# The split weights of four MLPs start at shifting places of their tiles

## The chip, the cores and the metric

One core of one Trainium2 chip runs the whole program. The metric is the device time of that core in microseconds. An execution before the change took 3301.78 and 3303.79 us in the two runs shown; the median is 3302.78 us.

## What is computed

The reference is a float32 network in two blocks on 512 latent tokens (and 256 context tokens in the first block) of 1024 features. The first block has two layers of mixed attention (grouped heads, low-rank heads, a pooling branch), each followed by a squared-relu MLP. The second block has a dilated-attention layer and a gated recurrence, each followed by the same kind of MLP. So there are four MLPs of this form:

```python
def sq_relu_mlp(h, w1, w2):
    return jnp.square(jax.nn.relu(h @ w1)) @ w2      # w1: 1024 x 4096, w2: 4096 x 1024
```

The MLP of the first layer works on 768 tokens, the other three on 512.

## The kernel before

**Products in two parts.** Each float32 operand is split into a high part (type fp32r, a rounded copy) and a low part (the difference). A product is three matmuls, `mm3` (lines 159 to 163): high by high (line 161), high by low (162), low by high (163), all summed in one PSUM bank.

**Weights.** `wcols` and `wchunk` bring a chunk of 128x2048 numbers: one DMA into a raw tile `wr`, a ScalarE copy into `wh` (line 187), a VectorE subtraction into `wl` (line 188). Each of `wr`, `wh` and `wl` has two buffers, so chunk n waits for the matmuls of chunk n-2 to leave its buffers and then has the time of chunk n-1 to be ready. The first two chunks after `self.cut = 2` are cut into kt/2 pieces.

**The MLP** (`mlp`, line 469). In the up stage a chunk holds 256 hidden features (eight blocks of 128 rows, 256 columns each). The weights are the stationary operand, loaded 128 by 128, and the tokens `t` stream past them as the moving operand. The result goes through Relu and Square on ScalarE and is split into the tiles `t` of the hidden features. In the down stage a chunk holds 512 rows and 512 output columns, and the roles are exchanged: 128 tokens of hidden features are stationary, the weights stream by 512 columns. Eight rounds of `ups`, two down chunks, `ups` make one MLP: 16 up chunks and 16 down chunks. In the profile's names the moving operand stands first: `b<-t,wh` is the up stage, `b<-wh,t` the down stage; `b` and `s` are two kinds of PSUM tiles (the second block has only `b`).

**Counts from the loops.** First MLP, 768 tokens: down 6 x 2 x 4 x 3 x 8 = 1152 matmuls of 512 columns; up 14 chunks x 2 x 8 x 3 = 672 of 512 and as many of 256, and for the first two chunks, whose tokens come in three runs of 256, 288 more of 256: 960 of 256. Each of the other three MLPs: 768 down and 672 up of 512 columns, 192 up of 256.

**Where the tiles lie.** The pools are laid out one behind the other along each partition. In bytes of a partition: the two buffers of `wl` begin at 33952 and 43168, those of `wh` at 52384 and 61600, those of `wr` at 70816 and 79008. All of these are 32 bytes past a multiple of 128. The general tiles `t` begin at 134848 + 6144 n in the first block, 64 past a multiple of 128, and at 113056 + 4096 n in the second, 32 past one. Within the MLPs every block of an operand starts whole multiples of 512 bytes behind its tile's start. So in the first block the starts of weights and tokens differ by 32 bytes (modulo 64) and in the second block by none.

Of the kernel before, what the change touches and what calls it, by code (L numbers as in the profile page):

```python
# [8 lines left out]
F32 = mybir.dt.float32  # L9
# [19 lines left out]
# ---------------------------------------------------------------- constants of the shapes  # L29
# [81 lines left out]
class Net:  # L111
    def __init__(self, ctx, tc, t, out):
        self.ctx, self.tc, self.nc, self.t, self.out = ctx, tc, tc.nc, t, out
        pool = lambda name, bufs, **kw: ctx.enter_context(tc.tile_pool(name=name, bufs=bufs, **kw))
        self.cst = pool("cst", 1)
        self.wp = pool("wp", 2)
        self.wk = pool("wk", 2)
        self.pb = self.ps = None
        self.nbank = 0
        self.pend = []  # L120
        self.nev = 0
        self.fill = []
        self.cut, self.aid = 0, self.nc.vector
        self.cols = {}

    # ------------------------------------------------------------ small helpers
# [38 lines left out]
    def raw(self, tag="wr"):  # L165
        return self.wp.tile([128, 2048 if tag == "wr" else 2304], F32, tag=tag, name=tag)

    def wchunk(self, segs, kt, n):
        """Weights [kt*128, n] gathered from column segments (part slice, k slice, column, source)."""
        nc = self.nc  # L170
        f = lambda x: x.rearrange("p (k n) -> p k n", k=kt)
        hi = self.wp.tile([128, 2304], F32R, tag="wh", name="wh")[:, :kt * n]
        lo = self.wp.tile([128, 2304], F32R, tag="wl", name="wl")[:, :kt * n]
# [17 lines left out]
    def wcols(self, w, cols, kt=8):  # L191
        """Weights [kt*128, sum] from column ranges of w."""
        segs, at = [], 0
        for c0, c1 in cols:
            src = w[:, c0:c1].rearrange("(k p) n -> p k n", p=128)
            segs.append((slice(0, 128), slice(0, kt), at, src))
            at += c1 - c0
        return self.wchunk(segs, kt, at)

    # work put off by a number of ticks, so that no engine's queue holds it before its operands are there  # L200
# [13 lines left out]
    def need(self, *keys):  # L214
        """Emits all that was put off up to the last of keys (all of it without keys)."""
# [3 lines left out]
    def only(self, key):  # L219
        """Emits what was put off under one key, ahead of the rest."""  # L220
# [15 lines left out]
    def rsqrt_act(self, st, scale, eps):  # L236
        """The same where the tables of ScalarE are not in use for exponentials."""
# [3 lines left out]
    def split_to(self, hi, lo, src):  # L241
        """src (SBUF, full precision) into its two parts."""
# [7 lines left out]
    # ------------------------------------------------------------ setup  # L250
    def setup(self):
# [34 lines left out]
        # the parts of a modulation's row stand two partitions apart  # L286
# [17 lines left out]
    def load_cols(self, names, eng):  # L304
        """Vectors of features as columns, turned from rows."""
# [23 lines left out]
    # ------------------------------------------------------------ modulation  # L329
    def mod_load(self, i, u, tag="wr"):  # L330
        """Columns u*256.. of layer i's modulation weights, by 128 rows."""
# [13 lines left out]
    def mod_rows(self, ps, raw, more=False):  # L345
        """Four partial sums of the two rows of a modulation, 32 partitions apart."""
# [5 lines left out]
    def row_parts(self, out, ps):  # L352
        """Rows of a modulation, their high parts on partitions r of 32 and the low ones on r + 2."""
# [4 lines left out]
    def mod_unit(self, i, u):  # L358
        """Columns u*256.. of layer i's modulation: rows for a gate, else turned to per-feature columns."""
# [32 lines left out]
    def affine(self, i, which):  # L392
        """Per-feature factor and shift of the modulated norm, [128, 8, 2 (latent, context)]."""
# [21 lines left out]
    # ------------------------------------------------------------ norm and turn  # L415
    def turn(self, n, xh, xl, c0, a=None, b=None, every=2):
        """n (two halves of [128 tokens, 512]) to [feature, token] columns c0.. of the pair tiles, with factor and shift."""
# [26 lines left out]
    def kx(x, k, c0, n, step=1):  # L444
        """k-th 128 features of pair tiles x = (hi, lo), columns c0.."""
# [4 lines left out]
    def ssq(self, x, hf, ss):  # L450
        """Sum of squares of half hf of x into ss[:, hf]."""
# [16 lines left out]
    # ------------------------------------------------------------ squared-relu MLP  # L468
    def mlp(self, width, xT, w1, w2, ranges, tiles, sink, lag=3):
        nc = self.nc  # L470
        self.cut = 2
# [14 lines left out]
        def chunk():  # L486
            """The next 256 hidden features: weights, and tiles of their parts."""
            c0 = len(hs) * 256
            hs.append((self.slot([128, 2, width], F32R), self.slot([128, 2, width], F32R)))
            return hs[-1], self.wcols(w1, [(c0, c0 + 256)])  # L490
# [16 lines left out]
        for g in range(8):  # L507
# [3 lines left out]
            for c, (tt, c0) in self.skew(tiles, lag if g == 7 else len(tiles)):  # L511
                if w[c] is None:
                    w[c] = self.wcols(w2[g * 512:(g + 1) * 512], [(c * 512, c * 512 + 512)], kt=4)
                    self.pump()
# [9 lines left out]
    def skew(tiles, lag):  # L524
        """(0, tile) and (1, tile) over the tiles, the second following the first by lag tiles."""
# [6 lines left out]
    # ============================================================ first block  # L532
# [3 lines left out]
    def gains(self, i):  # L536
        """Head gains on every partition."""
# [3 lines left out]
        n = 0  # L541
# [8 lines left out]
    def tables(self, at, eng):  # L550
        """Rope tables with the head gains folded in."""
# [23 lines left out]
    def rope(self, dst, ps, nh, tab, tt, tmp):  # L575
        """dst = gains and (for latent tokens, over the last rw columns) rotation of nh heads."""
# [16 lines left out]
    def heads(self, ps, nh, w, tab, tt, out, sq, t1, t2):  # L593
        """Normed, gained, rotated heads of ps [128, nh*w] into out [128, nh, w]."""
# [9 lines left out]
    # ------------------------------------------------------------ attention over all tokens  # L604
    def attention(self, i, jobs):
        """jobs: dicts of prep (emits what the job needs, returns (kind, q, k, v)), mix tile, fill steps."""
# [4 lines left out]
        def ring(tag, n, width, size):  # L611
            """Space n of a ring of size in the tiles of weights, which are taken as they are needed."""
# [68 lines left out]
        def emit(v, u):  # L681
            """Scores of unit v between the turns and products of unit u."""
# [35 lines left out]
    def mix_parts(self, j, m):  # L718
        """Half m of a pair of mixed features that was kept whole, into its parts."""
# [7 lines left out]
    # ------------------------------------------------------------ one layer  # L727
    def enter(self, i):
        """Tiles of layer i's input, and the step that fills a token tile of them from the residual."""
# [11 lines left out]
    def first(self, cols):  # L741
        """First layer: its input and the first projection, a quarter of the features at a time as their modulation
        comes in. Returns the input tiles and the projection's sums."""
# [47 lines left out]
        def units(s):  # L791
            """Rows of the modulation of quarter s."""
# [8 lines left out]
        def columns(s):  # L801
            """The modulation's columns of quarter s."""
# [19 lines left out]
        def features(s, tp):  # L822
            """The parts of the features of quarter s of a pair of token tiles."""
# [59 lines left out]
    def layer(self, i, xT, tab, sums=None):  # L883
# [32 lines left out]
        # ckv | kr | cq (first half)  # L916
# [20 lines left out]
        # cq (second half) | q heads 0 3  # L937
# [21 lines left out]
        # k heads | v heads  # L959
# [6 lines left out]
        # q heads 1 4 2 5  # L966
# [5 lines left out]
        def stacked(src, toks, hi, lo=None):  # L972
            """Pairs of heads turned into parts over both halves of the rows: hi with lo, or (hi, lo) each twice."""
# [16 lines left out]
        # pool input; meanwhile the keys of the heads that share them  # L990
# [28 lines left out]
        # second projections of the latent-rank heads, a pair of heads at a time  # L1019
# [97 lines left out]
        # output projection, gated into the residual  # L1117
# [8 lines left out]
        def weights(c):  # L1126
            """A quarter of the output projection's columns, rows as the mixed features lie."""
# [111 lines left out]
    # ============================================================ second block  # L1239
# [5 lines left out]
    def ln_rows(self, name, i):  # L1245
        """Gain and shift of a layer norm on every partition."""
# [13 lines left out]
    def ln_turn(self, j, name, i, rows, xT, wait=2, table=True):  # L1260
        """Layer norm of token tile j: to feature-major parts, and in place as the next residual."""
# [19 lines left out]
        def finish():  # L1281
            """The last norm of token tile j, out to memory."""
# [40 lines left out]
    def project_out(self, w, mT, name, i):  # L1323
        """Output projection and the norm after it. Returns a function for the product of the first 768 mixed features and
        a quarter of the columns with a token tile, one that ends a token tile and norms it, and the tiles it fills."""
# [59 lines left out]
    # ------------------------------------------------------------ dilated attention  # L1385
    def dilated(self, xT):
# [10 lines left out]
        def project(r, order):  # L1397
            """Steps that project, rotate and turn the four heads of round r, two pairs; the tiles they fill."""
# [71 lines left out]
        def scores(T, hh, j):  # L1470
            """Masked scores of a head and block, exponentials and the sums' reciprocals; both heads of a pair at once."""
# [70 lines left out]
        held = (0, 1), (1, 0), (1, 1)  # places of the last steps of a round's projection in the units of the round  # L1542
# [38 lines left out]
        def unit(r, u, put, fill):  # L1581
            """Scores of unit u, the turns of the unit before it, the products of the one before that; steps between."""
# [51 lines left out]
    # ------------------------------------------------------------ gated recurrence  # L1634
    def hgrn(self, xT):
# [13 lines left out]
        def gates(h, pz, pq, key, f, q):  # L1649
# [7 lines left out]
            # log f over the whole range of f: one of the two factors is 1  # L1657
# [19 lines left out]
        def recur(h, qd, kd, kp, dec, box):  # L1677
            """The stages of one head's recurrence."""
# [67 lines left out]
        # weights in the order of their use: inputs of the first pair of heads, then gates, queries and inputs of each  # L1746
# [64 lines left out]
    def lower_bounds(self, rows):  # L1811
        nc = self.nc
        # lower bounds: the softmax over the two layers, second minus nothing of the first
# [74 lines left out]
```

## Time and profile before

| | us |
|---|---|
| median of the runs shown (2) | 3302.78 |
| lowest, highest | 3301.78, 3303.79 |
| span of the profiled execution | 3301.2 |
| TensorE busy in it | 3238.5 (98%) |
| VectorE busy | 1776.6 (54%) |
| ScalarE busy | 1265.7 (38%) |
| first MLP, from 406.8 | 576.4 |
| second MLP, from 1257 | 361.0 |
| third MLP, from 2319.7 | 360.3 |
| fourth MLP, from 2933.8 | 358.7 |

The profiled execution is told by its span, from its first to its last instruction; the page gives no other time of it. Matmuls overlap in the pipeline, so the duration of one is longer than the step from its start to the next start, and a busy TensorE says little. The rate is read in the timeline, as the time between two starts divided by the number of matmuls between them.

### The profile page before, as it was taken

The page shows a single profiled execution, that of the slowest core. Times are in us where ns is not written, and L with a number is a line of the kernel's source. Part 1 is how long each engine was busy: PE and PEld are TensorE (multiplying, and loading weights), DVE is VectorE, ACT ScalarE, POOL GpSimd, SP SyncE. Part 2 cuts the span into 40 slices and gives each one's busy share as a digit, 9 for nine tenths or more (in the row PEclk, how much of TensorE's full clock was granted, in tenths as well). Part 3 has the DMA queues.
Part 4 walks back from the last instruction along what each step waited for, and adds up shares of the span by engine and source line. Part 5 has one row for each costly group of instructions (what it writes and reads, how often), then busy time and mean ns, then how long its engine had stood idle before and what let it go on. Part 6 is the DMA issues. An engine that isn't in the chain of part 4 may idle for free.

```text
span 3301.2 us, 52357 instructions
## 1 busy us (share of the span) xinstructions
PE 3238.5 (98%) x21704; PEld 2807.8 (85%) x21704; DVE 1776.6 (54%) x3550; ACT 1265.7 (38%) x2549; POOL 376.2 (11%) x541
## 2 busy tenths in 40 slices
PE   7999999999999999999999999999999999989998
PEld 6877988788889788888899999998888878888887
DVE  6677554444466866555644343435544467664445
ACT  4566432222236754222223333334322246542222
POOL 4343100000004420000000000001100030030000
PEclk9999999999999999999999999999999999999999
DMA  7132233333321022322321112112223222133332
GB/s 215 51 103 91 77 104 113 105 115 115 115 58 49 1 66 89 102 90 91 102 77 65 55 62 65 52 55 71 94 90 102 98 73 65 64 103 102 94 98 77
DMA packets 246509, 281.62 MB, mean 85 GB/s; under 512 B 19518, under 2 KB 208384, under 8 KB 246272
## 3 DMA queue, kind: packets, MB, share of 16 engines
q1 hardware_dynamic: 244528, 273.28, 26.0%
q10 hardware_dynamic: 1584, 4.98, 0.4%
q8 instruction: 171, 2.80, 0.4%
q14 instruction: 66, 0.54, 0.1%
q0 software_dynamic: 160, 0.02, 0.0%
HBM read 276.16 MB, written 2.10 MB: 84 GB/s over the span
## 4 chain that ended last, share of the span: by engine, by line
PE 80%; issue 11%; DVE 4%; ACT 2%; POOL 1%; DMA 1%; SPq 0%; ACTq 0%; DVEq 0%; POOLq 0%
PE b L161 18%; PE b L162 18%; PE b L163 18%; PE s L161 4%; PE s L163 4%; PE s L162 4%; PE b L671 2%; PE b L655 2%; PE b L349 1%; PE s L633 1%; DVE t L248 1%; DVE wl L188 1%; PE b L1529 1%; PE b L1445 1%; PE b L1526 1%
## 5 line engine op out<-in xcount | busy, mean ns | idle before, releaser
L161 PE MATMUL b<-wh,t 128*128 128x256 f32 (+2 forms) x2948 | 986.6, 335 | 1.5 <-ACT t L247 1.0
L162 PE MATMUL b<-wl,t 128*128 128x256 f32 (+2 forms) x2948 | 968.3, 328 | 3.9 <-DVE wl L188 3.9
L163 PE MATMUL b<-wh,t 128*128 128x256 f32 (+2 forms) x2948 | 968.8, 329 | 2.7 <-DVE t L248 2.7
L187 ACT ACTIVATE wh<-wr 128x2048 fp32r<-128x2048 f32 (+4 forms) x253 | 389.2, 1549 | 895.1 <-PE b L163 547.3
L188 DVE TENSOR_TENSOR wl<-wr,wh 128x2048 fp32r<-128x2048 f32 (+4 forms) x237 | 460.5, 1947 | 416.6 <-ACT wh L187 415.7
L161 PEld LDWEIGHTS b<-wh,t 128*128 128x128 f32 x2948 | 595.2, 202 | 53.8 <-issue 4.5
L162 PEld LDWEIGHTS b<-wl,t 128*128 128x128 f32 x2948 | 596.5, 202 | 44.3 <-DVE wl L188 4.5
L163 PEld LDWEIGHTS b<-wh,t 128*128 128x128 f32 x2948 | 595.9, 202 | 44.3 <-DVE t L248 3.5
L161 PE MATMUL b<-t,wh 128*128 128x512 f32 (+1 forms) x1232 | 440.8, 359 | 3.0 <-ACT t L247 3.0
L162 PE MATMUL b<-t,wh 128*128 128x512 f32 (+1 forms) x1232 | 439.4, 357 | 1.1 <-DVE t L248 1.1
L163 PE MATMUL b<-t,wl 128*128 128x512 f32 (+1 forms) x1232 | 439.1, 357 | 1.0 <-DVE wl L188 1.0
L161 PEld LDWEIGHTS b<-t,wh 128*128 128x128 f32 x1232 | 233.4, 190 | 39.7 <-ACT t L247 3.4
L163 PEld LDWEIGHTS b<-t,wl 128*128 128x128 f32 x1232 | 233.7, 190 | 35.6 <-DVE wl L188 1.4
L162 PEld LDWEIGHTS b<-t,wh 128*128 128x128 f32 x1232 | 233.7, 190 | 35.2 <-DVE t L248 1.6
L243 DVE CAST t<-h 128x512 fp32r<-128x512 f32 (+1 forms) x176 | 66.1, 377 | 241.2 <-ACT h L481 241.0
L480 ACT ACTIVATE h<-b 128x512 f32<-128x512 f32 (+1 forms) x138 | 70.8, 513 | 220.6 <-PE b L163 220.6
L1186 DVE TENSOR_TENSOR h<-b,gate 128x512 f32<-128x512 f32 (+1 forms) x141 | 89.0, 631 | 120.0 <-PE b L163 119.9
L161 PE MATMUL s<-wh,t 128*128 128x256 f32 (+2 forms) x428 | 146.8, 343 | 1.7 <-ACT h L927 1.0
L1321 DVE TENSOR_TENSOR xl<-xl,b 128x512 f32<-128x512 f32 x128 | 87.3, 683 | 111.3 <-PE b L163 111.3
L162 PE MATMUL s<-wl,t 128*128 128x256 f32 (+2 forms) x428 | 144.1, 337 | 0.0
L163 PE MATMUL s<-wh,t 128*128 128x256 f32 (+2 forms) x428 | 144.1, 337 | 0.0
L647 POOL TENSOR_SCALAR wl<-wl,st 128x768 f32<-128x768 f32 (+1 forms) x120 | 103.6, 864 | 160.6 <-DVE st L646 132.8
(363 smaller groups left out, 4515.5 us busy)
## 6 DMA issues: line engine op xcount, KB each, us to landing
wr<-in_w_mlp SPq DMA_DIRECT2D x64, 1024.0 KB, 5.3
wr<-in_w_mod SPq DMA_DIRECT2D x44, 1024.0 KB, 5.3
wr<-in_attn_w_in SPq DMA_DIRECT2D x36, 1024.0 KB, 5.0
wr<-in_ffn_w_up SPq DMA_DIRECT2D x32, 1024.0 KB, 5.4
wr<-in_ffn_w_down SPq DMA_DIRECT2D x32, 1024.0 KB, 5.0
wr<-in_hgrn_w_in SPq DMA_DIRECT2D x12, 1024.0 KB, 5.1
wr<-in_w_out SPq DMA_DIRECT2D x8, 640.0 KB, 5.1
wr<-in_w_in SPq DMA_DIRECT2D x4, 1024.0 KB
```

The costliest lines, as they stand in the source:

```text
L161: mm(out, a[0], b[0], start=start, stop=False)
L162: mm(out, a[0], b[1], start=False, stop=False)
L163: mm(out, a[1], b[0], start=False, stop=stop)
L187: nc.scalar.activation(hv, rv[:, k], AF.Copy)
L188: (self.aid if cut > 1 and m % 2 else nc.vector).tensor_sub(lv, rv[:, k], hv.bitcast(F32))
L243: self.nc.vector.tensor_copy(hi, src)
L480: nc.scalar.activation(r, ps, AF.Relu)
L647: nc.gpsimd.tensor_scalar(P[:, :n], P[:, :n], sm, 1.0, op0=ALU.mult, op1=ALU.mult)
L655: nc.tensor.transpose(ps[:, kk, a * 128:(a + 1) * 128], u["P"][e, a][:, k0:k0 + 128], self.ident)
L671: nc.tensor.matmul(u["O"][64 * e:64 * e + 64, :256], v[:, k, e * 64:(e + 1) * 64], u["PT"][e, k2][:, kk, :], start=(k == 0), stop=(k == u[ ...
L1186: nc.vector.tensor_mul(tmp, ps, g[:, c0:c0 + n])
L1321: self.nc.vector.tensor_add(x, x, ps)
```

## The change

A counter `nmlp` numbers the MLPs from 1. Each weight chunk of an MLP gets a place, `2 * n + nmlp % 2`, where n is the number of the chunk in its stage (0 to 15 in the up stage and again 0 to 15 in the down stage). `wh` and `wl` of that chunk begin that many 4 byte words behind the tile's start: odd places 1 to 31 in the first and third MLP, even places 0 to 30 in the second and fourth. The tiles `wh` and `wl` grow by 32 words to hold this. All other users of `wchunk` keep place 0. The raw tile, the DMAs, the number and shape of all instructions, and their order stay as they are. The two buffers of `wl` and of `wh` each grow by 128 bytes, so the second buffer of `wl` moves by 128 bytes, the two of `wh` by 256 and 384, and all that is laid out behind them by 512.

```diff
-        self.cut, self.aid = 0, self.nc.vector
+        self.cut, self.aid, self.nmlp = 0, self.nc.vector, 0
...
-        return self.wp.tile([128, 2048 if tag == "wr" else 2304], F32, tag=tag, name=tag)
+        return self.wp.tile([128, 2048 if tag == "wr" else 2336], F32, tag=tag, name=tag)
...
-    def wchunk(self, segs, kt, n):
+    def wchunk(self, segs, kt, n, at=0):
...
-        hi = self.wp.tile([128, 2304], F32R, tag="wh", name="wh")[:, :kt * n]
-        lo = self.wp.tile([128, 2304], F32R, tag="wl", name="wl")[:, :kt * n]
+        hi = self.wp.tile([128, 2336], F32R, tag="wh", name="wh")[:, at:at + kt * n]
+        lo = self.wp.tile([128, 2336], F32R, tag="wl", name="wl")[:, at:at + kt * n]
...
-    def wcols(self, w, cols, kt=8):
+    def wcols(self, w, cols, kt=8, place=0):
...
-        return self.wchunk(segs, kt, at)
+        return self.wchunk(segs, kt, at, place)
...
     def mlp(self, width, xT, w1, w2, ranges, tiles, sink, lag=3):
         nc = self.nc
+        self.nmlp += 1
+        place = lambda n: 2 * n + self.nmlp % 2
         self.cut = 2
...
-            return hs[-1], self.wcols(w1, [(c0, c0 + 256)])
+            return hs[-1], self.wcols(w1, [(c0, c0 + 256)], place=place(len(hs) - 1))
...
-                    w[c] = self.wcols(w2[g * 512:(g + 1) * 512], [(c * 512, c * 512 + 512)], kt=4)
+                    w[c] = self.wcols(w2[g * 512:(g + 1) * 512], [(c * 512, c * 512 + 512)], kt=4, place=place(2 * g + c))
```

The rest of the diff takes comments out.

## Rows read from the trace of the kernel before

**Rows 1.** The page: busy us by engine; granted clock in 40 slices.

```profile
PE 3238.5 (98%) x21704; PEld 2807.8 (85%) x21704; DVE 1776.6 (54%) x3550; ACT 1265.7 (38%) x2549; POOL 376.2 (11%) x541
...
PEclk9999999999999999999999999999999999999999
```

**Rows 2.** The page: chain that ended last, share of the span by engine.

```profile
PE 80%; issue 11%; DVE 4%; ACT 2%; POOL 1%; DMA 1%; SPq 0%; ACTq 0%; DVEq 0%; POOLq 0%
```

**Rows 3.** Busy time by stretch, first and third MLP: stretch, length, engines, clock, DMA.

```profile
406.80:983.20 576.40, 576.39 (x3251) 472.43 (x3250) 285.22 (x469) 156.93 (x264) 9.29 (x10) 1.00 0.33 105
...
2319.70:2680.00 360.30, 357.04 (x1666) 299.31 (x1665) 169.52 (x221) 114.58 (x146) 21.11 (x18) 0.99 0.28 92
```

**Rows 4.** Groups by line and shape, first MLP: down stage, line 161.

```profile
L161 PE MATMUL b<-wh,t 128*128 128x512 f32 x256 | 102.3, 400 | 0.0
...
L161 PE MATMUL s<-wh,t 128*128 128x512 f32 x128 | 51.3, 401 | 0.0
```

**Rows 5.** The same, third MLP: down, up by 512, up by 256; the weights' split.

```profile
L161 PE MATMUL b<-wh,t 128*128 128x512 f32 x256 | 99.9, 390 | 0.0
...
L161 PE MATMUL b<-t,wh 128*128 128x512 f32 x224 | 87.1, 389 | 0.0
...
L188 DVE TENSOR_TENSOR wl<-wr,wh 128x2048 fp32r<-128x2048 f32 x30 | 68.8, 2292 | 88.8 <-ACT wh L187 88.8
L187 ACT ACTIVATE wh<-wr 128x2048 fp32r<-128x2048 f32 x30 | 57.6, 1918 | 178.0 <-PE b L163 119.0 <-PE b L162 59.0
...
L161 PE MATMUL b<-t,wh 128*128 128x256 f32 x64 | 19.2, 309 | 1.5 <-ACT t L247 1.5
```

**Rows 6.** Timeline of TensorE, first block, down: start, us; 48 steps apart.

```profile
899.78 0.40 PE L162 MATMUL s<-wl,t 128*128 128x512 f32 x1
...
910.99 0.40 PE L162 MATMUL b<-wl,t 128*128 128x512 f32 x1
```

**Rows 7.** The same, second block, down; 49 steps apart.

```profile
2587.74 0.39 PE L162 MATMUL b<-wl,t 128*128 128x512 f32 x1
...
2598.85 0.39 PE L163 MATMUL b<-wh,t 128*128 128x512 f32 x1
```

**Rows 8.** The same, first block, up; 48 steps apart.

```profile
1363.62 0.40 PE L163 MATMUL s<-t,wl 128*128 128x512 f32 x1
...
1374.82 0.40 PE L163 MATMUL b<-t,wl 128*128 128x512 f32 x1
```

**Rows 9.** The same, second block, up; 49 steps apart.

```profile
2602.70 0.39 PE L162 MATMUL b<-t,wh 128*128 128x512 f32 x1
...
2613.81 0.39 PE L163 MATMUL b<-t,wl 128*128 128x512 f32 x1
```

**Rows 10.** The same, 256 columns, first MLP; 43 steps apart.

```profile
439.87 0.28 PE L162 MATMUL s<-t,wh 128*128 128x256 f32 x1
...
444.88 0.28 PE L163 MATMUL b<-t,wl 128*128 128x256 f32 x1
```

**Rows 11.** The same, 256 columns, second block's projections; 12 steps apart.

```profile
1645.05 0.28 PE L161 MATMUL b<-wh,t 128*128 128x256 f32 x1
...
1646.49 0.28 PE L161 MATMUL b<-wh,t 128*128 128x256 f32 x1
```

**Rows 12.** The same, stationary tokens taken 16 bytes apart; 10 steps apart.

```profile
1744.83 0.39 PE L163 MATMUL b<-wh,t 128*128 128x256 f32 x1
...
1747.17 0.39 PE L161 MATMUL b<-wh,t 128*128 128x256 f32 x1
```

**Rows 13.** The same, two passes of a plain float32 product.

```profile
188.67 0.59 PE L1042 MATMUL b<-wr,t 128*128 128x256 f32 x2
```

**Rows 14.** Groups by line and shape, whole span: such passes.

```profile
L1042 PE MATMUL b<-wr,t 128*128 128x256 f32 x72 | 21.6, 381 | 0.0
```

**Rows 15.** Waits of TensorE in the third MLP: engine, line, waited for, us, times.

```profile
PE b L422 <- DVE t L1303: 1.5, 2, 1.1
PE b L161 <- ACT t L247: 1.5, 1, 1.5
PE b L162 <- DVE t L248: 0.3, 1, 0.3
```

## The prediction, made before the changed kernel was run

> **What bounds the kernel now.** I read the page first. TensorE is busy for 98% of the span at the full granted clock [rows 1], and it carries 80% of the chain that ended last [rows 2]. Then the busy time by stretch: in the MLPs TensorE has no gap that counts [rows 3], and in the third MLP it waits 3.3 us in all, at the MLP's two ends [rows 15]. So an MLP lasts as long as its matmuls follow one another, and the question is the step from one matmul's start to the next.
>
> The timeline gives that step, and it has two values. In the first block, matmuls of 512 columns start 11.21 us / 48 = 233.5 ns apart in the down stage [rows 6] and 11.20 / 48 = 233.3 ns in the up stage [rows 8]. In the second block they start 11.11 / 49 = 226.7 ns apart, down and up [rows 7, 9]. Shape, type and clock are the same. With 256 columns the order is reversed: 5.01 / 43 = 116.5 ns in the first block [rows 10], 1.44 / 12 = 120.0 ns in the second [rows 11]. [...]
>
> What differs between the blocks is where the tiles lie. Weights and tokens start 32 bytes apart (modulo 64) in the first block and at like places in the second. It is the same step whether the weights are moving or stationary, so what counts seems to be how the two reads stand to each other. The trace cannot prove that: slots, PSUM tiles and larger distances differ too. But it is the only thing here on which the change acts.
>
> **The change, part by part.** No instruction is added, taken away or moved, and no queue gets anything new. What changes is the start of `wh` and `wl`, for all 32 chunks of each MLP. The affected matmuls, by the loops and the counts [rows 4, 5]: first block 1824 + 1440 = 3264 of 512 columns (the down part of the first MLP is (256 + 128) x 3 = 1152) and 960 + 192 = 1152 of 256; second block 2 x 3 x (256 + 224) = 2880 of 512 and 2 x 3 x 64 = 384 of 256.
>
> *The step, by the two values seen.* Places run through all distances modulo 64 bytes at an even spacing, so in each block some chunks get the good distance and some the bad one. With all 512 column steps of the first block at 226.7, the gain is 3264 x 6.7 = 21.9 us; with all of the second block at 233.4, the loss is 2880 x 6.7 = 19.3 us. With 256 columns the difference is 3.5 ns: at most 1152 x 3.5 = 4.0 lost in the first block and 384 x 3.5 = 1.3 gained in the second. No row shows a distance between, and I take the mean, since places sweep evenly and nothing favours an end: 512 columns, -3264 x 3.35 + 2880 x 3.35 = -10.9 + 9.6 = -1.3 us; 256 columns, +2.0 - 0.7 = +1.3 us. Together 0.
>
> *A start off the grid.* Before, all long reads started at a multiple of 32 bytes. Now most start elsewhere, and a run of words may need one more fetch at its ends. The nearest row is the dilated projection, whose stationary words lie 16 bytes apart: the step there is 2.34 / 10 = 234 ns for 128 words [rows 12], so one word fetched alone costs at most 234 / 128 = 1.8 ns. One such fetch for each of 6144 + 1536 = 7680 matmuls would be 14 us. The lower end is 0, or a gain as above. I take 3 us, half of what the 3456 down matmuls would pay (6.2): there the moving operand is shifted, and its read is what the step is made of, while a load of the up stage lies beside the matmul before it.
>
> [...]
>
> *The split.* The ScalarE copy takes 1.918 us and the VectorE subtraction 2.292 us [rows 5], both now writing to other places. I cost this at nothing: a chunk of the up stage gives TensorE 48 x 226.7 ns = 10.9 us and a down chunk as much, the split takes 4.2, and TensorE's waits name neither line 187 nor 188 [rows 15]. Even at twice the time it would fit. Only at the head of an MLP is the cover thin: 4 x 4.2 = 17 us if both doubled, with no row that suggests it. The DMAs still land at place 0.
>
> *The larger tiles.* Buffers move by 128 to 512 bytes. Starts already differed by multiples of 512 with no sign of it; a move by 128 alone is not seen. It would touch some 6400 matmuls of 256 columns outside the MLPs, at most 6400 x 3.5 = 22 us either way. I take 0, since their position modulo 64 and 128 is kept.
>
> Sum: 0 + 3 + 0 + 0 = +3 us on the span of 3301.2, which is 1.6 below the median of the runs. On the median: 3302.8 + 3 = 3306 us.
>
> **The rivals.** *Nothing happens.* The two steps may come from something that the change leaves alone (PSUM tiles, slots, the blocks' own layout). For it: the step is constant over whole MLPs although 16 different tiles `t` take part. Time: 3303. [...]
>
> *Faster.* The first block may suffer from one special distance, 32 bytes, and nearly every other place may be as good as the second block's. Against it: there are but two distances in the trace, and one good one proves nothing of the others. Time: 3302.8 - 21.9 = 3281.
>
> *Slower.* An operand that starts off its grid may be fetched word by word over its whole length. Where stationary, its load then costs what the strided loads cost, 234 ns a matmul: 256 columns, (1152 x 117.5 + 384 x 114) ns = 179 us, and 512 columns of the second block's up stage, 1344 x 7.3 ns = 10 us; together +189, 3492 us. Where moving, it would stream at the pace of plain float32: two passes of 256 columns take 0.59 us and one 0.381, so one step is 0.21 us [rows 13, 14], 0.42 for 512; 3456 x (420 - 230) ns = 657 us more. It decides from 66 / 7680 = 8.6 ns a matmul on. Against it: the strided loads start at 0, 4, 8 and 12 bytes into their grid in turn and show one step, but for them every word is alone anyhow, so this says little. A milder form, 3 to 8 ns a matmul, gives 3326 to 3364.
>
> **How the numbers follow.** The mixture, with its small price for the ends, gets 0.54; nothing happens 0.16; faster 0.13; slower 0.13; the remaining 0.04 is for the head of the MLPs, the moved buffers, and a distance better than any seen. Predicted: 3306. The lower end of the range is all good steps, 3302.8 - 21.9 - 1.3 = 3279.6; the upper end all bad ones with a fetch more in each, 3302.8 + 19.3 + 4.0 + 14 = 3340. It holds the first three cases, and leaves out most of the slower one and the rest. Two per cent, about what a measurement of this kernel can tell from no change, is 66 us: beyond 3369 lies most of the slower case and some of the rest, 0.12; below 3237 nothing that the rows offer, 0.01; between, 0.87.
>
> **What would show it.** The steps of the changed kernel should differ from chunk to chunk, between about 226 and 235 ns for 512 columns, in all four MLPs. If the first block stays at 233.4 and the second at 226.7 in every chunk, the first rival is right. If the first block is at 226.7 nearly throughout, the second is. Steps far above 235 in the odd places (first and third MLP) or in most chunks show the third. The split's durations should stay at 1.92 and 2.29 us, and the waits of TensorE should not name it. The prediction is wrong if the distance matters in a way that the two values do not span, or if a split that writes off its grid becomes late.

## The result, and the profile after

The changed kernel takes 3322.38 us (3321.07 to 3323.68, 2 runs) against 3302.78: a ratio of 1.0059, 95% interval 1.004 to 1.0078, which is 13 to 26 us more. 3306 had been forecast, with a range of 3279.6 to 3340.

The head of the page after shows the same picture as [rows 1, 2]: the same number of instructions, the granted clock in the top tenth in every slice (0.995 in the mean, before and after), TensorE at 98%, and its busy time 17.8 us longer.

```profile
span 3321.5 us, 52357 instructions
...
PE 3256.3 (98%) x21704; PEld 2813.3 (85%) x21704; DVE 1779.8 (54%) x3550; ACT 1265.2 (38%) x2549; POOL 373.8 (11%) x541
...
PEclk9999999999999999999999999999999999999999
...
PE 80%; issue 11%; DVE 4%; ACT 2%; POOL 1%; DMA 1%; SPq 0%; ACTq 0%; DVEq 0%; POOLq 0%
```

The busy time by stretch, after, for the four MLPs from their first to their last matmul; the columns are those of [rows 3].

```profile
407.96:986.75 578.79, 578.73 (x3251) 476.46 (x3249) 285.16 (x467) 156.41 (x264) 9.30 (x10) 1.00 0.33 104
1261.60:1621.65 360.05, 359.54 (x1649) 295.06 (x1647) 200.95 (x258) 108.28 (x134) 6.62 (x6) 1.00 0.31 97
2324.07:2692.40 368.33, 364.58 (x1666) 299.22 (x1665) 170.24 (x221) 114.59 (x146) 20.96 (x17) 1.00 0.27 90
2947.00:3313.10 366.10, 361.20 (x1649) 296.58 (x1647) 171.32 (x218) 108.00 (x130) 17.91 (x15) 1.00 0.27 87
```

Against 576.4, 361.0, 360.3 and 358.7 us before, the first MLP has lost 2.4, the second has won 1.0, and the two of the second block have lost 8.0 and 7.4: 16.8 of the 20.3 us by which the span grew. TensorE's waits and the weights' split in the third MLP are as in [rows 5, 15]. First the split's groups, after:

```profile
L189 DVE TENSOR_TENSOR wl<-wr,wh 128x2048 fp32r<-128x2048 f32 x30 | 68.8, 2294 | 90.5 <-ACT wh L188 90.5
L188 ACT ACTIVATE wh<-wr 128x2048 fp32r<-128x2048 f32 x30 | 57.5, 1917 | 184.7 <-PE b L163 123.9 <-PE b L162 60.7
```

And TensorE's waits in that stretch, after:

```profile
PE b L423 <- DVE t L1306: 1.5, 2, 1.0
PE b L161 <- ACT t L248: 1.5, 1, 1.5
PE b L162 <- DVE t L249: 0.8, 1, 0.8
```

So the time is in the step from matmul to matmul. In the timeline of TensorE after, these are the first and last start of six stretches, each of 45 steps within one chunk (columns: start us, us, engine, line):

```profile
1387.90 0.39 PE L162 MATMUL b<-wl,t 128*128 128x512 f32 x1
...
1398.11 0.39 PE L162 MATMUL b<-wl,t 128*128 128x512 f32 x1
...
1488.06 0.39 PE L162 MATMUL b<-wl,t 128*128 128x512 f32 x1
...
1498.68 0.40 PE L162 MATMUL b<-wl,t 128*128 128x512 f32 x1
...
2578.09 0.39 PE L162 MATMUL b<-t,wh 128*128 128x512 f32 x1
...
2588.30 0.39 PE L162 MATMUL b<-t,wh 128*128 128x512 f32 x1
...
2633.53 0.39 PE L162 MATMUL b<-wl,t 128*128 128x512 f32 x1
...
2644.30 0.40 PE L162 MATMUL b<-wl,t 128*128 128x512 f32 x1
...
2645.02 0.39 PE L162 MATMUL b<-wl,t 128*128 128x512 f32 x1
...
2655.32 0.39 PE L162 MATMUL b<-wl,t 128*128 128x512 f32 x1
...
3090.30 0.39 PE L162 MATMUL b<-wl,t 128*128 128x512 f32 x1
...
3100.92 0.40 PE L162 MATMUL b<-wl,t 128*128 128x512 f32 x1
```

Divided by 45 these are 226.9, 236.0, 226.9, 239.3, 228.9 and 236.0 ns; before there were only 233.4 in the first block and 226.7 in the second [rows 6 to 9]. The step now changes from chunk to chunk, from 226.7 to 239.9. What orders it within this trace is seen when each chunk is put beside the places of its operands. After the change `wl` begins at 33952 and 43296, `wh` at 52640 and 61984, and the tiles `t` 512 bytes later than before. Call **distance** the start of the stationary operand less that of the moving one, modulo 256 bytes. Where two blocks happen to have the same distance at even places, their mean steps over a chunk are the same, though tiles and PSUM differ:

| stage, distance | second MLP, ns | fourth MLP, ns |
|---|---|---|
| down, 72 | 231.49 | 231.49 |
| down, 88 | 235.98 | 235.96 |
| down, 136 | 234.68 | 234.74 |
| down, 192 | 228.90 | 228.90 |
| up, 24 | 231.17 | 231.17 |
| up, 176 | 230.21 | 230.21 |
| up, 192 | 229.04 | 229.04 |

(The second and the sixth stretch listed above are the row of distance 88.) Distance 0 gives 226.7 to 226.9, in the first block too: that is the first stretch, a chunk of the second MLP with place 8. It is not the only good one: the third stretch has 226.9 at another distance. Most other distances give 230 to 236. In the down stages the distance and the start of the moving operand change together, so this table alone cannot part the two. Modulo 256 the distances before were 32 (down) and 224 (up) in the first block and 0 in the second.

A second thing shows in the down stages, and most of all at odd places. Chunks whose weights, the moving operand there, start 4 bytes past a multiple of 16 average 237.3 ns over 939 steps, those 12 past it 229.9 over 931, those at 0 and 8 past it 231.7 and 233.5. The fourth and fifth stretch are two such neighbours, 4 and 12 past. In the up stages, where the weights are stationary, the same four groups average 231.7 to 233.3, without such an order.

### The profile page after: what moved, and what is told of

It is laid out like the page before. It is cut to its first block, busy times and chain, and to the rows that moved or that the text cites. A ratio compares the mean times of both kernels' runs of the same rounds, so it can differ in the third digit from the quotient of the medians.

```text
span 3321.5 us, 52357 instructions
## 1 busy us (share of the span) xinstructions
PE 3256.3 (98%) x21704; PEld 2813.3 (85%) x21704; DVE 1779.8 (54%) x3550; ACT 1265.2 (38%) x2549; POOL 373.8 (11%) x541
## 4 chain that ended last, share of the span: by engine, by line
PE 80%; issue 11%; DVE 4%; ACT 2%; POOL 1%; DMA 1%; SPq 0%; ACTq 0%; DVEq 0%; POOLq 0%
PE b L161 18%; PE b L163 18%; PE b L162 18%; PE s L161 4%; PE s L163 4%; PE s L162 4%; PE b L674 2%; PE b L658 2%; PE b L350 1%; PE s L636 1%; DVE t L249 1%; DVE wl L189 1%; PE b L1532 1%; PE b L1448 1%; PE b L1529 1%
## 5 line engine op out<-in xcount | busy, mean ns | idle before, releaser
L161 PEld LDWEIGHTS b<-t,wh 128*128 128x128 f32 x1232 | 233.4, 190 | 42.0 <-ACT t L248 3.4
L163 PEld LDWEIGHTS b<-t,wl 128*128 128x128 f32 x1232 | 233.4, 189 | 38.4 <-DVE wl L189 1.2
```

Source lines behind the costliest of these rows:

```text
L161: mm(out, a[0], b[0], start=start, stop=False)
L163: mm(out, a[1], b[0], start=False, stop=stop)
```

## Experiments

The edits below are shown against the changed kernel. The theory to test is that the step follows from the distance modulo 256. Its rivals: that the weights' own start counts, that something else slows the first block, and that the larger tiles are harmless or, on the contrary, the whole cost. One more rival needs no run: that the writes of the weights' split slow TensorE's reads. In the up stage of the second MLP before, the step averages 233.2 ns while a split runs and 233.4 ns while ScalarE, VectorE and GpSimd are all idle; in the third MLP it is 226.8 and 226.7. So the level of the step does not come from those writes. The DMAs land where they did in all runs with tiles of the old size. In the expectations a 16 byte line stands for a multiple of 16 bytes in a start address, by which the four groups above are told apart; the runs show nothing further behind it.

**e1_tiles_only.** The tiles grow, the places stay 0.

```diff
-        place = lambda n: 2 * n + self.nmlp % 2
+        place = lambda n: 0
```

> All places 0; only the tiles wh and wl keep the 32 more words, so the second buffer of each moves by 128 bytes (modulo 256) against the tokens. Distance theory (the step of a matmul follows from the start of the stationary operand less that of the moving one, modulo 256 bytes): in the second block every second chunk goes from distance 0 to 128, which the trace of the changed kernel shows at 233.26 ns against 226.7, so 1440 matmuls of 512 columns lose 6.6 ns, +9 us; the first block goes from distances 32 and 224 to 96 and 160 in half of its chunks, 233.3 in both, 0 us; with what lies outside the MLPs some 3312 us, between 3309 and 3316. Rival (as predicted, a buffer that keeps its place modulo 128 costs nothing): 3303 us, all steps as before. Rival (the places themselves, off a 16 byte line, are the cost): 3303 us too.

Measured: 3314.34 against 3303.81 us, ratio 1.003 (1.002 to 1.0041), +7 to +14 us. In the timeline of the third MLP, two down chunks behind one another, 45 steps each, in the two buffers:

```profile
2405.11 0.39 PE L162 MATMUL b<-wl,t 128*128 128x512 f32 x1
...
2415.31 0.39 PE L162 MATMUL b<-wl,t 128*128 128x512 f32 x1
...
2415.99 0.39 PE L162 MATMUL b<-wl,t 128*128 128x512 f32 x1
...
2426.49 0.40 PE L162 MATMUL b<-wl,t 128*128 128x512 f32 x1
```

226.7 and 233.3 ns: the buffer that has not moved against the tokens keeps its step, the one moved by 128 bytes does not. Both start at the same place modulo 128 as before. So the larger tiles are not harmless, and the period is not 128 or less.

**e3_places_only.** The places of the change in tiles of the old size.

```diff
-        return self.wp.tile([128, 2048 if tag == "wr" else 2336], F32, tag=tag, name=tag)
+        return self.wp.tile([128, 2048 if tag == "wr" else 2304], F32, tag=tag, name=tag)
...
-        hi = self.wp.tile([128, 2336], F32R, tag="wh", name="wh")[:, at:at + kt * n]
-        lo = self.wp.tile([128, 2336], F32R, tag="wl", name="wl")[:, at:at + kt * n]
+        hi = self.wp.tile([128, 2304], F32R, tag="wh", name="wh")[:, at:at + kt * n]
+        lo = self.wp.tile([128, 2304], F32R, tag="wl", name="wl")[:, at:at + kt * n]
```

> The places of the change, but tiles of 2304 words as before, so no buffer moves. Distance theory: summed over all chunks from the steps that the trace of the changed kernel shows for each distance (a third of the distances interpolated), the MLPs take 15 us more than before: second block +11 to +14, first block about 0 to +3; 3318 us, between 3312 and 3322. Rival (the moved buffers are most of the 20 us): under 3310 us. Rival (off-line starts alone): about the full 20 us, 3322.

Measured: 3320.28 against 3303.81 us, ratio 1.0049 (1.0036 to 1.0063). The places alone cost 16.5 us, the tiles alone some 10, both together 20: the parts do not add, since each takes the second block from its good distance and it can be lost only once. The second block's 512 column stages take 671.2 us here, 663.5 in e1, 654.5 before and 671.4 after the change. The total lies between the theory's 3318 and the 3322 of the rival that starts off a multiple of 16 bytes are the whole cost, so it does not part them.

Chunk by chunk the trace shows more. Here no buffer has moved, so every distance is known, and both blocks again agree with each other: 230.0 ns at distance 208 in the down stage, 233.3 at 192. But the changed kernel had 233.3 at 208 and 228.9 at 192. The first two lines are a down chunk of the fourth MLP at distance 192, the other two an up chunk of the second MLP at distance 16, 45 steps each:

```profile
3164.82 0.40 PE L162 MATMUL b<-wl,t 128*128 128x512 f32 x1
...
3175.32 0.40 PE L162 MATMUL b<-wl,t 128*128 128x512 f32 x1
...
1373.15 0.39 PE L162 MATMUL b<-t,wh 128*128 128x512 f32 x1
...
1383.65 0.40 PE L162 MATMUL s<-t,wh 128*128 128x512 f32 x1
```

Both are 233.3 ns. So the distance modulo 256 orders the steps within one layout and does not fix them across layouts. Between the two kernels `wh` also moved against `wl`, from a multiple of 512 bytes apart to an odd multiple of 256; whether that is the reason was not tested. The forecast for this run came right in its total although some of the steps behind it did not.

**e4_place_one.** Tiles of the old size, one place for all chunks; the step expected of each stage was read off the trace of the changed kernel.

```diff
-        place = lambda n: 2 * n + self.nmlp % 2
+        place = lambda n: 1
```

> Tiles of 2304 words, place 1 (4 bytes) for all chunks of all MLPs. Distance theory, chunk by chunk the same: first block up, distance 228: 226.7 ns (before 233.3); second block up, distance 4: 232.5 (before 226.7); second block down, distance 252 with the moving operand 4 past a 16 byte line: 237.4 (before 226.7); first block down, distance 28, such a start too: not seen yet, between 233 and 240. In all about 3328 us, between 3320 and 3333. Rival (the start of the weights alone counts): both up stages have one step, and both down stages have one step.

Measured: 3327.77 us (one run). The timeline shows the second MLP's up stage, the third's up stage and its down stage, 94 matmuls of each:

```profile
1321.64 0.39 PE L162 MATMUL s<-t,wh 128*128 128x512 f32 x1
...
1342.72 0.39 PE L162 MATMUL s<-t,wh 128*128 128x512 f32 x1
...
2387.52 0.39 PE L162 MATMUL b<-t,wh 128*128 128x512 f32 x1
...
2409.12 0.40 PE L162 MATMUL b<-t,wh 128*128 128x512 f32 x1
...
2409.82 0.41 PE L162 MATMUL b<-wl,t 128*128 128x512 f32 x1
...
2431.92 0.40 PE L162 MATMUL b<-wl,t 128*128 128x512 f32 x1
```

Over 93 steps these are 226.7, 232.3 and 237.6 ns, against 226.7, 232.5 and 237.4 expected; the first block's down stage, for which only 233 to 240 had been foretold, is at 236.8. The two up stages have the same weights' start and unlike steps, so the weights' start alone does not decide.

**e2_distance_zero.** Distance 0 in all four MLPs, tiles of the old size.

```diff
-        place = lambda n: 2 * n + self.nmlp % 2
+        place = lambda n: 8 * (self.nmlp < 3)
```

> Tiles as before (2304 words), place 8 (32 bytes) for all chunks of the two MLPs of the first block and 0 in the second block: every operand pair of the four MLPs then starts at distance 0 modulo 256. Distance theory: the 3264 matmuls of 512 columns of the first block step at 226.7 instead of 233.3 ns, -21.5 us, and the 1152 of 256 columns at 119.6 instead of 117 to 118, +2 us: 3283 us, between 3280 and 3286. Rival (the first block is slower through its PSUM tiles, slots or layout): 3303 us with steps of 233.3. Rival (only a weight start on its own grid counts, not the distance): 3303 us.

Measured: 3288.45 against 3303.81 us, ratio 0.9954 (0.994 to 0.9967). In the timeline of the second MLP, down, 93 steps:

```profile
1331.51 0.39 PE L162 MATMUL b<-wl,t 128*128 128x512 f32 x1
...
1352.59 0.39 PE L162 MATMUL b<-wl,t 128*128 128x512 f32 x1
```

226.7 ns, in the block that had 233.4 before. So nothing else holds the first block at 233.4. Here its operands start a multiple of 512 bytes apart, and those of the second block, at the same step, an odd multiple of 256: so at distance 0 a period of 256 is enough. The time missed the expected 3280 to 3286: the gain is 15.4 us and not 20. The two MLPs' 512 column stages fall from 765.5 to 745.7 us and their 256 column stages rise from 136.1 to 139.3. In the first MLP other matmuls lie between its own (before, its own were 2784 of the 3251 in that stretch [rows 3]). Its mean step falls from 235.0 to 229.1 ns in the down stage and from 234.9 to 229.4 in the up stage: 1.7 and 1.6 ns above 233.3 before, 2.4 and 2.7 above 226.7 here, so that part did not get shorter with the step.

**e6_zero_and_projections.** As e2, with the dilated layer's weights 32 bytes on: for 256 columns distance 0 is not the good one.

```diff
-                wc = self.wcols(w, [(c0, c0 + 256)])
+                wc = self.wcols(w, [(c0, c0 + 256)], place=8)
```

> As e2_distance_zero, and the weights of the dilated layer's input projection (256 columns, weights moving) at place 8 too, distance 224 instead of 0. In the first MLP before, 256 columns step at 116.8 ns at distance 224 and in the second block at 119.6 to 120 at distance 0. Distance theory: 2688 matmuls of that projection (the 768 with strided tokens aside) gain 2.8 ns, -7.5 us against e2_distance_zero: 3281 us, between 3277 and 3286. Rival (256 columns are slower in the second block for another reason): 3288 us, as e2_distance_zero.

Measured: 3280.43 against 3305.12 us, ratio 0.9928 (0.9915 to 0.9942). It beats both kernels of the case. In the timeline of that projection, where [rows 11] showed 120.0 ns, 28 steps:

```profile
1643.67 0.28 PE L163 MATMUL b<-wh,t 128*128 128x256 f32 x1
...
1646.93 0.28 PE L161 MATMUL b<-wh,t 128*128 128x256 f32 x1
```

This is 116.4 ns, as in the first block's 256 column stage [rows 10].

**e5_both_shifted.** Is it the distance alone? Tiles have the old size, and the other three MLPs keep place 0. The second MLP's up stage has distance 0, and in its down stage both operands go g words further in round g, at distance 0 throughout.

```diff
-        place = lambda n: 2 * n + self.nmlp % 2
+        place = lambda n, down=False: (self.nmlp == 2) * (8 + down * (n // 2))
...
-            hs.append((self.slot([128, 2, width], F32R), self.slot([128, 2, width], F32R)))
+            s = (self.nmlp == 2) * (len(hs) // 2)
+            hs.append((self.slot([128, 2, width], F32R)[:, :, s:], self.slot([128, 2, width], F32R)[:, :, s:]))
...
+                    w[c] = self.wcols(w2[g * 512:(g + 1) * 512], [(c * 512, c * 512 + 512)], kt=4, place=place(2 * g + c, True))
```

> Tiles of 2304 words; only the second MLP (first block, 512 tokens in slots for 768) is changed. Its up stage has place 8, distance 0. In round g (0 to 7) of its down stage the hidden features of chunks 2g and 2g+1 begin g words behind their slots' start, and the weights at place 8 + g, so the distance is 0 in all rounds while both operands start 0, 4, 8 to 28 bytes behind a multiple of 64. Distance theory in its plain form: every round steps at 226.7 ns, as does the up stage; 768 + 672 matmuls gain 6.6 ns, -9.5 us, some 3294 us. Rival (a moving operand that starts off a 16 byte line costs by itself): rounds 0 and 4 at 226.7 and the others above it, odd rounds between 229 and 240 as the down stages of odd places in the changed kernel; some 3298 us.

Measured: 3301.08 us (one run; before 3305.12), above the 3294 of the theory and the 3298 of its rival. The steps decide, and the distance theory in its plain form falls. Rounds 0, 1 and 4 of that stage in the timeline:

```profile
1295.69 0.39 PE L162 MATMUL b<-wl,t 128*128 128x512 f32 x1
...
1316.77 0.39 PE L162 MATMUL b<-wl,t 128*128 128x512 f32 x1
...
1339.22 0.40 PE L162 MATMUL b<-wl,t 128*128 128x512 f32 x1
...
1361.34 0.40 PE L162 MATMUL b<-wl,t 128*128 128x512 f32 x1
...
1471.42 0.39 PE L161 MATMUL b<-wh,t 128*128 128x512 f32 x1
...
1493.04 0.39 PE L162 MATMUL b<-wl,t 128*128 128x512 f32 x1
```

These are 226.7, 237.8 and 230.0 ns (93, 93 and 94 steps). The eight rounds have 226.7, 237.8, 231.9, 229.0, 230.0, 235.9, 233.8 and 229.6. The rival missed one point: round 4, whose operands start on a multiple of 16, was to be at 226.7 and is at 230.0.

**e7_stationary_shifted.** As e5, with the weights of the down stage left at place 8: only the stationary operand is shifted.

```diff
-        place = lambda n, down=False: (self.nmlp == 2) * (8 + down * (n // 2))
+        place = lambda n, down=False: (self.nmlp == 2) * 8
```

> As e5_both_shifted, but the weights of the second MLP stay at place 8 in the down stage too. The moving operand then starts at a multiple of 64 in every round and only the stationary one is g words behind, so the distance is 4 g bytes. If the start that costs in e5 is the moving one, the rounds step as the up stages do at the same distance, where the stationary operand is shifted as well: 226.7 in round 0, 232.4 in round 1 (distance 4), 231.7 in round 2 (8), 233.0 in round 5 (20), 231.2 in round 6 (24), 233.4 in round 7 (28); in all some 3300 us. Rival (the start of the stationary operand is what cost in e5): round 1 at 237 or more and round 5 at 235 or more.

Measured: 3296.73 us (one run; before 3304.22). Rounds 1 and 3 in the timeline, 92 steps each:

```profile
1337.32 0.39 PE L162 MATMUL b<-wl,t 128*128 128x512 f32 x1
...
1358.70 0.40 PE L161 MATMUL b<-wh,t 128*128 128x512 f32 x1
...
1425.33 0.39 PE L162 MATMUL b<-wl,t 128*128 128x512 f32 x1
...
1446.18 0.39 PE L161 MATMUL b<-wh,t 128*128 128x512 f32 x1
```

Round 1 steps at 232.4, round 3 at 226.6. All rounds: 226.7, 232.4, 230.7, 226.7, 226.7, 233.3, 231.1, 232.3. Round 1 is where the up stages put distance 4, not at the 237.8 of e5, and rounds 5 and 6 are within 0.3 ns of the up stages as well; rounds 2 and 7 are 1.0 and 1.1 below. So at distances 4, 20 and 24 the stationary operand costs what it costs in the up stages, and what e5 showed beyond that is best put down to the start of the moving one. A stationary operand that starts 12 bytes past a multiple of 16 costs nothing here (round 3).

Round 4 does not fit. Its distance is 16, for which the expectation named no step, and it is at 226.7, where the up stages of e3 have 233.3 at distance 16 in both blocks. In the second MLP even the starts modulo 256 are the same there, with weights and tokens in exchanged roles. At distance 8 e3's up stage has 230.7, as round 2. So distance and moving start together do not give every step; what else enters stays open.

## Why the prediction was right, and which step was off

**The bound: right.** The MLPs last as long as their matmuls follow one another: the steps, summed below, change by 16.9 us, and the four MLPs by 16.8.

**What sets the step: the places, right and now shown; how they set it, only in part.** e1, e2 and e4 move the step between 226.7 and 237.6 ns by places alone, at the same instructions, so the rival that nothing happens is out. The prediction reckoned the distance modulo 64, which is too short: a move by 128 takes 226.7 to 233.3 in e1. Modulo 256 it orders the steps within a layout; e3 and e7 show that it is not all. And the steps reach 239.9 ns, beyond the 226 to 235 foretold, so the two values of before do not span what places can do.

**The step that failed is "I take the mean, since places sweep evenly and nothing favours an end".** For 512 columns it gave -10.9 us in the first block and +9.6 in the second. Measured, summed over the starts of all those matmuls: 765.5 to 764.5 us, -1.0, and 654.5 to 671.4, +16.9. The two values of before were not two ends of an even spread. 226.7 is what a few distances give; the sweep came to between 231.8 and 233.9 ns in each stage of the three MLPs of 512 tokens (without the six steps over 260 ns, 263 to 1395), whichever value the block had before. The second block sat on a good distance and could only lose. The time still lies in the range because its upper end had put all steps of that block at the bad value, +19.3; the forecast itself was 16 us low.

**The 256 column term was right:** +2.3 and -1.3 us measured for +2.0 and -0.7.

**A start off the grid, taken at 3 us: the mechanism was wrong, and its size came out by luck.** Weights 4 bytes past a multiple of 16 cost some 4 to 6 ns a matmul more when they move than those 0 and 8 past it (237.3 against 231.7 and 233.5), and those 12 bytes past it (229.9) are faster than those on it; an extra fetch of 1.8 ns at the ends, the bound then taken, explains neither. The two kinds nearly cancel: odd places average 233.6 ns and even ones 232.6, by estimate some 2 us over the 1920 down matmuls of the first and third MLP. In e5 the slow starts 4 past and the faster ones 12 past recur after 16 bytes (237.8 and 235.9 ns, 229.0 and 229.6). But it is not a matter of being off a multiple of 16: 12 past is as far off it as 4 past, and the start on a multiple of 16 that is none of 32 costs 3.3 ns (230.0 against 226.7). The heavy form, a whole read word by word, did not come: no chunk stood above 239.9 ns. The half that was charged to the down stages rests on the moving operand's read being what the step is made of; that was the author's estimate, and no run shows what a step is made of. That loads lie beside matmuls is seen in [rows 3]: 472.43 us of loads in the 576.40 us of the first MLP, of which matmuls fill 576.39.

**The split: right** (1.917 and 2.294 us after), no wait of TensorE in the four MLPs names it.

**The larger tiles: wrong.** They were costed at nothing because the places modulo 64 and 128 are kept; e1 prices them at some 10 us when they come alone. The prediction looked for their cost in the 256 column matmuls outside the MLPs; it lies in the second block's 512 column steps, 654.5 us before and 663.5 in e1. In the sum with the places they are largely covered, as above.

**Outside the MLPs** the span grew by 3.5 us, forecast as 0. e1, with the same moved buffers, shows none of it: from the first to the last matmul of each MLP, 1643.4 us lie outside, against 1644.1 before and 1647.6 after. Nor is it clear of scatter. In e2, e5, e6 and e7 nothing ahead of the first MLP is changed, and it begins at 406.7 to 408.5 us. So no cause is shown or needed. Open is why these distances and starts are the good ones: the runs show which they are in these layouts, not what makes them so.

## What to carry to other kernels

Where TensorE is the bound and its matmuls follow one another, put the step of each stage beside the start addresses of its two operands before looking for other causes. Two kernels or two blocks with the same instructions and unlike steps are a hint that a few bytes of padding are worth a try: here 32 bytes in three places were worth 0.7%. A distance that was good in one layout has to be measured again in the next: the changed kernel and e3 differ at the same distances, 228.9 against 233.3 ns at 192. And a sample of two values says nothing of what lies between: take one as the rule and the other as the exception, in both ways, before taking their mean.

## What was not expected of the hardware

- The step of a 128x128 by 512 fp32r matmul, stationary operands changing each time, ranges from 226.7 to 239.9 ns with nothing but start addresses changed, at a mean granted clock of 0.994 to 0.997 in every profiled run.
- With the moving operand on a multiple of 32 bytes, distances of 0, 12 and 16 bytes modulo 256 give 226.7 ns in the down stage (e7), 228 gives it in the up stage (e4), 128 gives 233.3 in the down stage (e1) and 16 gives 233.3 in the up stage (e3).
- The same distance and place can differ between layouts: 192 in the down stage is 228.9 ns in the changed kernel and 233.3 in e3.
- At distance 0, moving starts of 0, 4, 8, 12, 16, 20, 24 and 28 bytes past a multiple of 64 give 226.7, 237.8, 231.9, 229.0, 230.0, 235.9, 233.8 and 229.6 ns (e5).
- For 256 columns the order differs: in the second block's projections distance 0 gives 120.0 ns [rows 11] and distance 224 gives 116.4 (e6).
